# Right half of row blocks 2 and 3 as a streamed Strassen pair, with later loads of blocks 8 and 9 and a re-ordered second group

## Chip, cores, metric

One core of one Trainium2 chip. The metric is the device time of one execution in microseconds (us), as median over several executions. "Fast runs" are the undisturbed ones; all runs told of here are of that state, with every core's granted TensorE clock between 0.977 and 0.994.

## The reference

```python
def reference(a, b, gamma, eps):          # a, b: 2048 x 2048 float32, gamma: 2048
    x = np.matmul(a, b)
    rms = np.sqrt(np.mean(x ** 2, axis=-1, keepdims=True) + eps)
    return (gamma * x / rms).astype(np.float32)
```

The kernel works on 16 row blocks of 128 rows. Each row block of the output is finished only when all its 2048 columns exist, because the root mean square needs the whole row.

## The kernel before

The kernel has three phases.

1. **Streams.** A of row blocks 0 to 3 and the left half of B come in; each B block is used as it lands (first stream). Then the right half of B comes in the same way (second stream). Both are plain products.
2. **Strassen groups.** From row block 4 on, two row blocks form a group, and the group's left and right halves of 1024 columns each take seven products instead of eight. A product is 8 matmuls of 512 columns. While a group is computed, the next two row blocks of A are prepared: loaded, normed and scaled to fp16, transposed by DMA.
3. The last group is ordered by hand.

The parts that matter here:

```python
    def row_norm(mb):                       # ScalarE, 2.57 us
        for h in range(2):
            nc.scalar.activation(out=junk, in_=a32[mb][:, h * HALF:(h + 1) * HALF],
                                 func=ACTF.Square, scale=2.0 ** -8, accum_out=n2[:, h:h + 1])
        nc.scalar.activation(out=norm[mb], in_=n2[:, 0:1], func=ACTF.Sqrt, ...)
    # row_factor(mb): four small VectorE operations on norm[mb]
    # row_apply(mb):  a16 = a32 * factor, ScalarE for mb >= 6 (1.99 us); then transpose_dma(mb)
    # finish(mb):     VectorE: out = x * r * gamma, two half rows of 1.24 us, each stored by DMA

    def group_half(g, j, hooks):
        ...                                 # x11 .. x22: the four 512-column parts of the output
        t = x22
        at_hook(0)
        p2, p5 = new_bank(), new_bank()
        product(g, j, 2, p2)
        c = spare if (g, j) == (G0, 0) else t
        nc.scalar.copy(out=c, in_=p2)       # "the first copy"
        last_squares()
        at_hook(1)
        product(g, j, 5, p5)
        nc.vector.tensor_tensor(out=t, in0=p5, in1=c, op=ALU.add)
        at_hook(2)
        p1 = new_bank()
        product(g, j, 1, p1)
        ...
        at_hook(3)
        product(g, j, 4, p2, start=False)   # accumulates on p2: has to wait for the first copy
        nc.scalar.copy(out=x21, in_=p2)
        ...                                 # products 3, 7, 6 with hooks 4 to 7

    def hooks_of(g, j):                     # g == 2 is the first group, nxt = 2 * g + 2
        if j == 0:
            if g == G0: ...
            else:
                done = [2 * g - 2, 2 * g - 1]
                hook(0, row_factor, nxt)
                hook(1, apply, nxt)
                if g == G0 + 1:
                    hook(2, finish, r3)
                    done.insert(0, r3)
                for mb in done:
                    hook(1, take_rms, mb)
                hook(1, row_norm, nxt + 1)
                hook(2, row_factor, nxt + 1)
                hook(4 if g == G0 + 1 else 3, finish, 2 * g - 2)
                hook(4, apply, nxt + 1)
        else:
            ...
            if g + 2 < NG:
                hook(0, load_after, g, nxt + 2)     # waits for the first half's last sum
                hook(0, load_block, nxt + 3)
                hook(5, row_norm, nxt + 2)          # ahead of the next group's first copy
```

A hook is a place between two products at which the listed calls are issued. "Block 8" means row block 8 of A, and "scaling" a block is `row_apply`. The A sums are VectorE's sums of quarters of two row blocks of A; products 1, 2, 5, 6 and 7 of a group read them, so they need both blocks' transposes.

## Time and profile before

| | before |
|---|---|
| median | 224.36 us (224.12 to 224.77) |
| span of the profiled execution | 222.6 us, clock 0.993 |
| PE (TensorE matmul) busy | 211.1 us, 95% |
| DVE (VectorE) / ACT (ScalarE) busy | 73% / 58% |
| chain that ended last | PE 83%, DMA 8% |

The timeline of PE before, some of its rows. The columns are start, length, engine, source line, operation, output and input tiles, shape and count; a bracket at the end tells the idle time ahead of it and what ended it. A row without a bracket began as soon as the one before it let it.

```profile
24.69 1.67 PE L350 MATMUL acc<-b,head_at 128*128 128x512 bf16 x7 [0.44 <-DMA b<-in_b_dram]
...
69.25 3.62 PE L279 MATMUL acc<-b,s 128*128 128x512 bf16 x16
...
109.17 1.89 PE L279 MATMUL acc<-early,s 128*128 128x512 bf16 x8
110.90 3.62 PE L279 MATMUL acc<-early,head_at 128*128 128x512 bf16 x16
114.35 7.07 PE L279 MATMUL acc<-b,s 128*128 128x512 bf16 x32
```

The bracket at 24.69 is the last one; from there TensorE never waits. The first Strassen group starts at 69.25. The row at 110.90 is product 4 of the second group's right half: it follows its predecessor without a wait (it counts 16 matmuls because product 3 follows at once and stands in the same row).

ScalarE before, in the same stretch:

```profile
93.92 1.06 ACT L209 ACTIVATE sq<-a 128x1024 bf16<-128x1024 f32 x1 [1.33 <-DMA a<-in_a_dram]
...
96.49 0.57 ACT L498 COPY x<-acc 128x512 f32<-128x512 f32 x1
...
98.34 1.99 ACT L231 ACTIVATE head_at<-a,s 128x2048 f16<-128x2048 f32 x1
100.23 0.37 ACT L318 ACTIVATE rms<-tot 128x1 f32<-128x1 f32 x3
100.51 1.04 ACT L209 ACTIVATE sq<-a 128x1024 bf16<-128x1024 f32 x1
...
107.64 0.59 ACT L498 COPY x<-acc 128x512 f32<-128x512 f32 x1
```

The norm of block 8 (L209) waits for its load, but stands ahead of the first copy (L498 at 96.49). Scaling block 8 (L231 at 98.34) has no idle time ahead of it. The second half's first copy ends at 108.23, 2.7 us before product 4 needs it. That is the slack of this order.

### The profile page before, as it was taken

The page shows a single profiled execution, that of the slowest core. Times are in us where ns is not written, and L with a number is a line of the kernel's source. Part 1 is how long each engine was busy: PE and PEld are TensorE (multiplying, and loading weights), DVE is VectorE, ACT ScalarE, POOL GpSimd, SP SyncE. Part 2 cuts the span into 40 slices and gives each one's busy share as a digit, 9 for nine tenths or more (in the row PEclk, how much of TensorE's full clock was granted, in tenths as well). Part 3 has the DMA queues.
Part 4 walks back from the last instruction along what each step waited for, and adds up shares of the span by engine and source line. Part 5 has one row for each costly group of instructions (what it writes and reads, how often), then busy time and mean ns, then how long its engine had stood idle before and what let it go on. Part 6 is the DMA issues. An engine that isn't in the chain of part 4 may idle for free.

```text
span 222.6 us, 3026 instructions
## 1 busy us (share of the span) xinstructions
PE 211.1 (95%) x1043; PEld 98.6 (44%) x1043; DVE 161.8 (73%) x324; ACT 129.1 (58%) x272; POOL 24.5 (11%) x49
## 2 busy tenths in 40 slices
PE   7899999999999999999999999999999999999950
PEld 2445444444454444444444444444444444444430
DVE  2427557983999989978949298837994589587692
ACT  3110002807698895799646985699478954334570
POOL 7534232300000001000100002000200000000000
PEclk9999999999999999999999999999999999999997
DMA  6999999999973499818889259945994794044045
GB/s 184 223 202 209 203 208 211 212 303 259 327 280 159 188 272 292 310 72 226 276 228 400 58 174 222 366 151 143 246 368 168 97 282 189 0 188 193 0 190 188
DMA packets 36176, 47.13 MB, mean 212 GB/s; under 512 B 21952, under 2 KB 26048, under 8 KB 34496
## 3 DMA queue, kind: packets, MB, share of 16 engines
q0 software_dynamic: 9648, 23.33, 41.6%
q1 hardware_dynamic: 26080, 22.29, 33.0%
q10 hardware_dynamic: 432, 1.31, 2.0%
q8 instruction: 8, 0.13, 0.2%
q14 instruction: 8, 0.07, 0.1%
HBM read 34.60 MB, written 16.78 MB: 231 GB/s over the span
## 4 chain that ended last, share of the span: by engine, by line
PE 83%; DMA 8%; DVE 2%; POOL 2%; issue 1%; ACT 1%; DVEq 0%; ACTq 0%; POOLq 0%
PE acc L279 63%; PE acc L350 18%; DMA b<-in_b_dram 8%; POOL early L106 1%; DVE x L617 1%; POOL b L100 1%; DVE x L620 1%; PE tbank L179 1%; PE tbank L382 1%; PE tbank L165 1%; ACT sq L291 0%; DVEq L732 0%; ACT sq L682 0%; DVE x L690 0%; DVE r L322 0%
## 5 line engine op out<-in xcount | busy, mean ns | idle before, releaser
L279 PE MATMUL acc<-b,s 128*128 128x512 bf16 x376 | 83.3, 379 | 0.0
L279 PEld LDWEIGHTS <-s 128*128 128x128 f16 x472 | 46.2, 98 | 55.7 <-DVE s L244 0.2
L350 PE MATMUL acc<-b,head_at 128*128 128x512 bf16 x240 | 55.1, 379 | 0.6 <-DMA b<-in_b_dram 0.4
L291 ACT ACTIVATE sq<-x 128x512 bf16<-128x512 f32 x62 | 39.1, 631 | 10.9 <-DVE x L520 5.1
L340 DVE SCALAR_TENSOR_TENSOR x<-x,r,gamma_sb 128x1024 f32<-128x1024 f32 x28 | 34.7, 1282 | 0.8
L209 ACT ACTIVATE sq<-a 128x1024 bf16<-128x1024 f32 x24 | 25.4, 1057 | 16.8 <-DMA a<-in_a_dram 16.4
L350 PEld LDWEIGHTS <-head_at 128*128 128x128 bf16 x240 | 22.9, 98 | 26.7 <-issue 1.1
L393 ACT COPY x<-acc 128x512 f32<-128x512 f32 x11 | 5.9, 591 | 25.1 <-PE acc L350 25.1
L231 ACT ACTIVATE head_at<-a,s 128x2048 f16<-128x2048 f32 x10 | 19.9, 1990 | 0.0
L279 PEld LDWEIGHTS <-at_even 128*128 128x128 f16 x96 | 9.4, 98 | 11.5 <-issue 0.4
L279 PEld LDWEIGHTS <-head_at 128*128 128x128 f16 x96 | 9.4, 98 | 11.3
L100 POOL DMA_DIRECT2D b<-in_b_dram x15 | 10.6, 708 | 16.0 <-DMA b<-in_b_dram 13.2
L217 DVE TENSOR_SCALAR s<-norm 128x1 f32<-128x1 f32 x12 | 1.8, 150 | 14.3 <-ACT norm L212 14.2
L244 DVE TENSOR_TENSOR s<-at_even 128x1024 f16<-128x1024 f16 x15 | 9.7, 684 | 2.8 <-DMA at_even<-head_at 2.8
L291 ACT ACTIVATION_READ_ACCUMULATOR sq<-x 128x1 f32 x62 | 11.7, 188 | 0.0
L279 PE MATMUL acc<-t_left,s 128*128 128x512 bf16 x48 | 11.3, 379 | 0.0
L279 PE MATMUL acc<-early,s 128*128 128x512 bf16 x48 | 11.3, 379 | 0.0
L279 PE MATMUL acc<-early,at_even 128*128 128x512 bf16 x48 | 11.0, 379 | 0.0
L279 PE MATMUL acc<-t_left,at_even 128*128 128x512 bf16 x48 | 10.9, 379 | 0.0
L509 ACT COPY x<-acc 128x512 f32<-128x512 f32 x10 | 5.7, 575 | 8.9 <-PE acc L279 8.9
L279 PE MATMUL acc<-t_left,head_at 128*128 128x512 bf16 x48 | 10.8, 379 | 0.0
L279 PE MATMUL acc<-early,head_at 128*128 128x512 bf16 x48 | 10.8, 379 | 0.0
(86 smaller groups left out, 205.8 us busy)
## 6 DMA issues: line engine op xcount, KB each, us to landing
out_dram<-x SPq DMA_DIRECT2D x30, 512.0 KB, 3.1
a<-in_a_dram POOLq DMA_DIRECT2D x12, 1024.0 KB, 8.5
b<-in_b_dram POOLq DMA_DIRECT2D x15, 512.0 KB, 17.1
early<-in_a_dram POOLq DMA_DIRECT2D x7, 256.0 KB, 14.8
early<-in_b_dram ACTq DMA_DIRECT2D x2, 512.0 KB, 5.9
gamma_sb<-in_gamma_dram POOLq DMA_DIRECT2D x1, 1024.0 KB, 19.9
out_dram<-x SPq DMA_DIRECT2D x3, 256.0 KB, 3.5
early<-in_a_dram SPq DMA_DIRECT2D x1, 512.0 KB, 5.7
```

Of the source, the lines that this page charges most:

```text
L100: nc.gpsimd.dma_start(out=raw[j][kp], in_=b[kp * W2:(kp + 1) * W2, j * HALF:(j + 1) * HALF].rearrange("(t p) n -> p t n", p=P))
L106: nc.gpsimd.dma_start(out=ah(kp), in_=a[0:HB * P, kp * W2:(kp + 1) * W2].rearrange("(r p) k -> p r k", p=P))
L165: nc.tensor.matmul(view[:, t, r, :], ah(kp)[:, r, t * P:(t + 1) * P], identity, is_transpose=True, start=(t == 0 and r == 0), stop=(t == 1 ...
L209: nc.scalar.activation(out=junk, in_=a32[mb][:, h * HALF:(h + 1) * HALF], func=ACTF.Square, scale=2.0 ** -8, accum_out=n2[:, h:h + 1])
L231: nc.scalar.activation(out=a16[mb], in_=a32.pop(mb), func=ACTF.Copy, scale=factor.pop(mb))
L244: nc.vector.tensor_tensor(out=s_sum[s], in0=x, in1=y, op=op)
L279: nc.tensor.matmul(bank, lhsT[:, kp, :], rhs, start=(start and kp == 0), stop=(kp == KP - 1), skip_group_check=not start)
L291: nc.scalar.activation(out=sq[:, 0:CH], in_=src, func=ACTF.Square, scale=inv_sqrt_n, accum_out=msq[mb][:, c:c + 1])
L340: nc.vector.scalar_tensor_tensor(out=x, in0=x, scalar=r, in1=gamma_sb[:, h * HALF:(h + 1) * HALF], op0=ALU.mult, op1=ALU.mult)
L350: nc.tensor.matmul(bank, head_at[:, kt, r, :], head_rhs(c, kt), start=(kt == 0), stop=(kt == KT - 1))
L393: copy(out=x_chunk(*g), in_=banks[g])
L509: nc.scalar.copy(out=x21, in_=p2)
```

## The change

Its intent: save eight matmuls. Row blocks 2 and 3 times the right half of B become one Strassen pair, streamed with B: products 2, 5 and 1 are computed block by block as B lands, products 4, 3, 7, 6 after that. To make room, other work is moved:

- all of B is loaded ahead of A of blocks 4, 5;
- the pair's last sums and more finishes fall into the first group, so row block 2 is finished later;
- the loads of blocks 8, 9 wait for row block 2's scaling, not for the first half's last sum;
- block 8's norm, factor and scaling stand in the second group, behind its first copy; its factor stands behind row block 3's finish on VectorE.

The core of the diff (the streaming itself, many buffers and small moves are cut):

```diff
-    groups2 = [(r, c) for r in range(HB) for c in (2, 3)][:-1]
+    plain = [(r, c) for r in range(2) for c in (2, 3)]
+    ...
+    def stream_right(kp):                    # 8 plain matmuls and 3 of the pair per B block
+        ...
+    product(PAIR, 1, 4, pair[2], start=False)
+    product(PAIR, 1, 3, pair[5], start=False)
+    product(PAIR, 1, 7, p7, within={5: [lambda: turn(HB, 0)]})
+    product(PAIR, 1, 6, p6)
@@ group_half
-        t = x22
+        first = (g, j) == (G0, 0)
+        c, t = spare if first else (x22, x22)     # spare: now two buffers, one is t_first
@@ load_after
-        wait_for(x_chunk(2 * g + 1, 1)[:, 0:1])
+        wait_for(x_slot[r2][:, 0:1] if g == G0 else x_chunk(2 * g + 1, 1)[:, 0:1])
@@ hooks_of, second group, left half
+            elif g == G0 + 1:
+                hook(1, row_norm, nxt)
+                for mb in (r3, 2 * g - 2, 2 * g - 1):
+                    hook(1, take_rms, mb)
+                hook(2, finish, r3)
+                hook(2, row_factor, nxt)
+                hook(2, apply, nxt)
+                hook(2, row_norm, nxt + 1)
+                hook(3, row_factor, nxt + 1)
+                hook(4, finish, 2 * g - 2)
+                hook(4, apply, nxt + 1)
@@ hooks_of, right half
-                hook(0, load_after, g, nxt + 2)
-                hook(0, load_block, nxt + 3)
-                hook(5, row_norm, nxt + 2)
+                hook(2 if g == G0 else 0, load_after, g, nxt + 2)
+                hook(2 if g == G0 else 0, load_block, nxt + 3)
+                if g > G0:
+                    hook(5, row_norm, nxt + 2)
```

More of the change, by code (lines that the diff above doesn't have):

```diff
@@ L50 @@
     sq_pool = ctx.enter_context(tc.tile_pool(name="sq_pool", bufs=1))
-    stat_pool = ctx.enter_context(tc.tile_pool(name="stat_pool", bufs=8))
+    stat_pool = ctx.enter_context(tc.tile_pool(name="stat_pool", bufs=4))
+    msq_pool = ctx.enter_context(tc.tile_pool(name="msq_pool", bufs=8))
     ps_t = ctx.enter_context(tc.tile_pool(name="ps_t", bufs=1, space=bass.MemoryType.PSUM))
@@ L75 @@
     x_slot = [consts.tile([P, HALF], FP32, name=f"x_{n}") for n in range(8)]
-    spare = head_at.rearrange("p t r m -> p (t r m)")[:, K:2 * K].bitcast(FP32)[:, 0:CH]
+    spare = head_at.rearrange("p t r m -> p (t r m)")[:, K:2 * K].bitcast(FP32)
+    spare = [spare[:, 0:CH], consts.tile([P, CH], FP32, name="t_first")]
     def a16_slot(mb):
-        if mb < HB + 2:
-            return x_slot[HB + 1 + 2 * (mb % 2)].bitcast(FP16)
         flat = head_at.rearrange("p t r m -> p (t r m)").bitcast(FP16)
@@ L111, with load_half @@
     a32 = {}
+    def load_half(mb, h):
+        if h == 0:
+            a32[mb] = a_pool.tile([P, K], FP32, name="a32")
+        nc.gpsimd.dma_start(out=a32[mb][:, h * HALF:(h + 1) * HALF],
+                            in_=a[mb * P:(mb + 1) * P, h * HALF:(h + 1) * HALF])
     def load_block(mb):
@@ L123 @@
     load_head(1)
-    identity_f = consts.tile([P, P], FP32, name="identity_f")
+    identity_f = t_left[:, 2, KP - 1, 0:2 * P].bitcast(FP32)
     make_identity(nc, identity_f)
@@ L129 @@
     nc.vector.memset(warm, 0.0)
+    nc.vector.memset(pace, 1.0)
+    nc.scalar.activation(out=pace, in_=pace, func=ACTF.Sqrt)
     identity = consts.tile([P, P], BF16, name="identity")
@@ L172, with transpose_half @@
     a16 = {}
-    def transpose_half(mb, g):
-        bank = ps_t.tile([P, CH], FP32, name="tbank")
+    def transpose_half(mb, g, own_bank):
+        if own_bank:
+            bank = ps_t.tile([P, CH], FP32, name="tbank")
+        else:
+            bank = ps_a.tile([P, CH], FP32, name="acc")
         view = bank.bitcast(FP16).rearrange("p (g m) -> p g m", m=P)
@@ L182, in transpose_half, with take_transposed @@
             )
-        nc.vector.tensor_copy(out=at(mb)[:, g * 8:(g + 1) * 8, :], in_=view)
+        return view
+    def take_transposed(mb, g, view, copy):
+        copy(out=at(mb)[:, g * 8:(g + 1) * 8, :], in_=view)
     def transpose_dma(mb):
@@ L192, in new_msq @@
     def new_msq(mb):
-        msq[mb] = stat_pool.tile([P, NCH + 1], FP32, name="msq")
+        msq[mb] = msq_pool.tile([P, NCH + 1], FP32, name="msq")
         n_sq[mb] = 0
@@ L197 @@
         new_msq(mb)
+        nc.gpsimd.memset(msq[mb][:, NCH - 1:NCH], 0.0)
         nc.gpsimd.memset(msq[mb][:, NCH:], float(eps))
@@ L235, in quarter, with sum_of, a_sums @@
     def quarter(g, r, c):
+        if g < G0:
+            return head_at[:, c::2, 2 * g + r, :]
         return at(2 * g + r)[:, c::2, :]
-    def a_sums(g, which):
+    def sum_of(g, s):
+        return s_sum[s].bitcast(BF16) if g < G0 else s_sum[s]
+    def a_sums(g, which, lo=0, hi=KP):
         a11, a12, a21, a22 = (quarter(g, r, c) for r in range(2) for c in range(2))
@@ L243, in a_sums @@
             x, y, op = terms[s]
-            nc.vector.tensor_tensor(out=s_sum[s], in0=x, in1=y, op=op)
+            nc.vector.tensor_tensor(out=sum_of(g, s)[:, lo:hi, :], in0=x[:, lo:hi, :],
+                                    in1=y[:, lo:hi, :], op=op)
     def b_quarter(j, kp, r, c):
@@ L254, in b_sums @@
             nc.vector.tensor_tensor(out=sums[j][:, n, kp, :], in0=x, in1=y, op=op)
-    def b_sum_7(j, kp):
-        b21, b22 = (b_quarter(j, kp, 1, c) for c in range(2))
-        nc.vector.tensor_tensor(out=b21, in0=b21, in1=b22, op=ALU.add)
-    def b_sum_6(j, kp):
-        b11, b12 = (b_quarter(j, kp, 0, c) for c in range(2))
-        nc.vector.tensor_tensor(out=b12, in0=b12, in1=b11, op=ALU.add)
     def b_sums_in_place(j, kp):
@@ L270, in b_sums_in_place, with product_matmul, product @@
                                 op=ALU.add)
-    def product(g, j, m, bank, start=True):
-        for kp in range(KP):
-            lhsT = {3: quarter(g, 0, 0), 4: quarter(g, 1, 1)}[m] if m in (3, 4) else s_sum[m]
-            rhs = {1: lambda: sums[j][:, 0, kp, :], 2: lambda: b_quarter(j, kp, 0, 0),
-                   3: lambda: sums[j][:, 1, kp, :], 4: lambda: sums[j][:, 2, kp, :],
-                   5: lambda: b_quarter(j, kp, 1, 1), 6: lambda: b_quarter(j, kp, 0, 1),
-                   7: lambda: b_quarter(j, kp, 1, 0)}[m]()
-            nc.tensor.matmul(bank, lhsT[:, kp, :], rhs,
-                             start=(start and kp == 0), stop=(kp == KP - 1),
-                             skip_group_check=not start)
+    def product_matmul(g, j, m, bank, kp, start=True):
+        lhsT = {3: quarter(g, 0, 0), 4: quarter(g, 1, 1)}[m] if m in (3, 4) else sum_of(g, m)
+        rhs = {1: lambda: sums[j][:, 0, kp, :], 2: lambda: b_quarter(j, kp, 0, 0),
+               3: lambda: sums[j][:, 1, kp, :], 4: lambda: sums[j][:, 2, kp, :],
+               5: lambda: b_quarter(j, kp, 1, 1), 6: lambda: b_quarter(j, kp, 0, 1),
+               7: lambda: b_quarter(j, kp, 1, 0)}[m]()
+        nc.tensor.matmul(bank, lhsT[:, kp, :], rhs,
+                         start=(start and kp == 0), stop=(kp == KP - 1),
+                         skip_group_check=not start)
+    def product(g, j, m, bank, start=True, within={}):
+        for kp in range(KP):
+            for work in within.get(kp, ()):
+                work()
+            product_matmul(g, j, m, bank, kp, start)
     x_half = {}
@@ L291, in square, with square_half @@
         nc.scalar.activation(out=sq[:, 0:CH], in_=src, func=ACTF.Square,
+                             scale=inv_sqrt_n, accum_out=msq[mb][:, c:c + 1])
+    def square_half(mb, h):
+        c = n_sq[mb]
+        n_sq[mb] += 1
+        sq = sq_pool.tile([P, 2 * CH], BF16, name="sq")
+        nc.scalar.activation(out=sq, in_=x_tile(mb, h), func=ACTF.Square,
                              scale=inv_sqrt_n, accum_out=msq[mb][:, c:c + 1])
@@ L332, in rows @@
         return out[mb * P:(mb + 1) * P, lo:hi]
+    inverse_of = {}
     def finish(mb, order=(0, 1)):
-        if mb not in rms_of:
-            take_rms(mb)
-        r = inverse(rms_of.pop(mb))
+        if mb not in inverse_of:
+            if mb not in rms_of:
+                take_rms(mb)
+            inverse_of[mb] = inverse(rms_of.pop(mb))
+        r = inverse_of[mb]
         for h in order:
@@ L354, in new_bank @@
         return ps_a.tile([P, CH], FP32, name="acc")
-    later = ([("b", kp) for kp in range(5)]
-             + [("a", HB), ("b", 5), ("b", 6), ("a", HB + 1), ("b", 7)])
+    later = [("b", kp) for kp in range(KP)] + [("a", n) for n in range(4)]
     def load_later(n):
@@ L361, in load_later @@
             kind, which = later.pop(0)
-            load_b(1, which) if kind == "b" else load_block(which)
+            load_b(1, which) if kind == "b" else load_half(HB + which // 2, which % 2)
     def stream(groups, kp, before=(), when=None):
@@ L393, in evict @@
             copy(out=x_chunk(*g), in_=banks[g])
+    PAIR = G0 - 1
     groups1 = [(r, c) for r in range(HB) for c in range(2)][:-1]
@@ L399 @@
         x_tile(r, 0)
+    early_sums = {4: ((2,), 0, 6), 5: ((5,), 0, 7), 6: ((1,), 0, KP)}
     transpose_first()
@@ L406 @@
         before = [lambda: transpose_head(kp + 1)] if kp + 1 < KP else []
+        if kp in early_sums:
+            before.append(lambda: a_sums(PAIR, *early_sums[kp]))
         stream(groups1, kp, before, len(groups1) + 5 if kp == 0 else None)
@@ L412 @@
             b_sums(0, kp - 1)
+        if 0 < kp < KP - 2:
+            b_sums_in_place(0, kp - 1)
     load_later(2)
-    b_sums(0, KP - 1)
-    def prepare(mb):
-        row_norm(mb)
-        row_factor(mb)
-        row_apply(mb)
-    def b_sums_2(kp):
-        b_sums_in_place(0, kp)
-        b_sums(1, kp)
-        if kp + 1 < KP:
-            b_sum_7(1, kp)
-    r3 = HB - 1
-    squares = groups1 + [last1]
-    groups2 = [(r, c) for r in range(HB) for c in (2, 3)][:-1]
+    squares = groups1 + [last1]
@@ new lines, with pair_matmul @@
+    plain = [(r, c) for r in range(2) for c in (2, 3)]
+    pair = {}
+    def pair_matmul(m, kp):
+        if kp == 0:
+            pair[m] = new_bank()
+        product_matmul(PAIR, 1, m, pair[m], kp)
+    def stream_right(kp):
+        order = [(g, kt) for kt in (2 * kp, 2 * kp + 1) for g in plain]
+        if kp in (0, KP - 1):
+            order.sort(key=lambda x: plain.index(x[0]))
+        if kp == KP - 1:
+            for m in (2, 5):
+                pair_matmul(m, kp)
+            pair_matmul(1, kp - 1)
+        for g, kt in order:
+            if kt == 0:
+                banks[g] = new_bank()
+            head_matmul(banks[g], *g, kt)
+        if kp < KP - 1:
+            for m in (2, 5):
+                pair_matmul(m, kp)
+            if kp > 0:
+                pair_matmul(1, kp - 1)
+        else:
+            pair_matmul(1, kp)
@@ L431 @@
     for kp in range(KP):
         load_later(1)
-        before = [lambda: transpose_half(HB, 0)] if kp == 6 else []
-        if kp == 7:
-            before = [lambda: transpose_half(HB, 1)]
-        stream(groups2, kp, before)
+        b_sums(1, kp)
+        stream_right(kp)
         square(squares[kp][0], x_chunk(*squares[kp]))
-        if kp == 4:
-            prepare(HB)
-        if kp == 6:
-            prepare(HB + 1)
-        elif kp == KP - 1:
-            b_sums_in_place(0, kp - 1)
-        else:
-            b_sums_2(kp)
+        if kp > 0:
+            b_sums_in_place(1, kp - 1)
@@ L447 @@
+        if kp == 0:
+            b_sums(0, KP - 1)
+            b_sums_in_place(0, KP - 3)
+        if kp == 1:
+            b_sums_in_place(0, KP - 2)
+            b_sums_in_place(0, KP - 1)
+        if kp == 2:
+            a_sums(PAIR, (2,), 6, KP)
+            a_sums(PAIR, (5,), 7, KP)
+        if kp in (3, 4):
+            a_sums(PAIR, ((7, 6)[kp - 3],))
     nc.gpsimd.dma_start(out=gamma_sb, in_=gamma.partition_broadcast(P))
@@ L449, with turn, pair_sums, pair_ends @@
     load_block(HB + 3)
-    def squares2(r):
-        for c in (2, 3):
-            square(r, x_chunk(r, c))
-    evict(groups2[0:2], ())
-    squares2(0)
-    evict(groups2[2:-1], ())
-    bank = new_bank()
-    for kt in range(KT):
-        if kt in (0, 6):
-            transpose_half(HB + 1, kt // 6)
-            if kt == 0:
-                b_sums(1, KP - 2)
-                b_sum_7(1, KP - 2)
-        head_matmul(bank, r3, 3, kt)
-    evict(groups2[-1:], ())
-    row_norm(HB + 2)
-    a_sums(G0, (2, 5, 1))
-    finish(0, (1, 0))
-    b_sums_2(KP - 1)
-    nc.scalar.copy(out=x_chunk(r3, 3), in_=bank)
-    squares2(1)
+    r2, r3 = HB - 2, HB - 1
+    for r in range(HB):
+        x_tile(r, 1)
+    x11, x12, x21, x22 = (x_chunk(r, c) for r in (r2, r3) for c in (2, 3))
+    nc.scalar.copy(out=x22, in_=pair[2])
+    nc.vector.tensor_tensor(out=x22, in0=pair[5], in1=x22, op=ALU.add)
+    evict(plain, (2, 3))
+    b_sums_in_place(1, KP - 1)
+    product(PAIR, 1, 4, pair[2], start=False)
+    row_norm(HB)
+    row_norm(HB + 1)
+    nc.vector.tensor_tensor(out=x22, in0=pair[1], in1=x22, op=ALU.subtract)
+    row_factor(HB)
+    product(PAIR, 1, 3, pair[5], start=False)
+    row_apply(HB)
+    nc.scalar.copy(out=x21, in_=pair[2])
+    row_factor(HB + 1)
+    row_apply(HB + 1)
+    p7 = new_bank()
+    turned = {}
+    def turn(mb, g):
+        turned[mb, g] = transpose_half(mb, g, g == 0)
+    product(PAIR, 1, 7, p7, within={5: [lambda: turn(HB, 0)]})
+    turn(HB, 1)
+    for g in range(2):
+        take_transposed(HB, g, turned[HB, g], nc.scalar.copy)
+    nc.scalar.copy(out=x12, in_=pair[5])
+    p6 = new_bank()
+    product(PAIR, 1, 6, p6)
+    a_sums(G0, (5,))
+    for g in range(2):
+        turn(HB + 1, g)
+        take_transposed(HB + 1, g, turned[HB + 1, g], nc.vector.tensor_copy)
+    square_half(0, 1)
+    square_half(1, 1)
+    take_rms(0)
+    a_sums(G0, (2, 1))
+    def pair_sums():
+        nc.vector.tensor_tensor(out=x11, in0=x22, in1=x21, op=ALU.add)
+        nc.vector.tensor_tensor(out=x22, in0=x22, in1=x12, op=ALU.add)
+    def pair_ends():
+        nc.vector.tensor_tensor(out=x11, in0=p7, in1=x11, op=ALU.add)
+        nc.vector.tensor_tensor(out=x22, in0=p6, in1=x22, op=ALU.add)
     late = []
@@ L491, in group_half @@
         x11, x12, x21, x22 = (x_chunk(ra, c1), x_chunk(ra, c2), x_chunk(rb, c1), x_chunk(rb, c2))
-        t = x22
+        first = (g, j) == (G0, 0)
+        c, t = spare if first else (x22, x22)
         at_hook(0)
         p2, p5 = new_bank(), new_bank()
-        product(g, j, 2, p2)
-        c = spare if (g, j) == (G0, 0) else t
-        nc.scalar.copy(out=c, in_=p2)
+        one, two = ((5, p5), (2, p2)) if first else ((2, p2), (5, p5))
+        product(g, j, *one)
+        nc.scalar.copy(out=c, in_=one[1])
         last_squares()
         at_hook(1)
-        product(g, j, 5, p5)
-        nc.vector.tensor_tensor(out=t, in0=p5, in1=c, op=ALU.add)
+        product(g, j, *two)
+        nc.vector.tensor_tensor(out=t, in0=two[1], in1=c, op=ALU.add)
         at_hook(2)
@@ L550, in hooks_of @@
             if g == G0:
-                hook(0, row_factor, nxt)
-                hook(1, row_norm, nxt + 1)
-                hook(1, apply, nxt)
+                hook(0, finish, 0, (1,))
+                hook(1, row_norm, nxt)
+                hook(1, take_rms, 1)
+                hook(2, row_factor, nxt)
+                hook(2, finish, 0, (0,))
+                hook(2, apply, nxt)
+                hook(2, row_norm, nxt + 1)
                 hook(2, a_sums, g, (7, 6))
+                hook(2, finish, 1, (1, 0))
                 hook(2, row_factor, nxt + 1)
-                hook(2, finish, 1)
-                hook(3, squares2, 2)
+                hook(2, pair_sums)
+                hook(2, pair_ends)
                 hook(4, apply, nxt + 1)
-                hook(4, finish, 2)
-                hook(6, b_sum_7, 1, KP - 1)
+                hook(7, square_half, r2, 1)
+            elif g == G0 + 1:
+                hook(1, row_norm, nxt)
+                for mb in (r3, 2 * g - 2, 2 * g - 1):
+                    hook(1, take_rms, mb)
+                hook(2, finish, r3)
+                hook(2, row_factor, nxt)
+                hook(2, apply, nxt)
+                hook(2, row_norm, nxt + 1)
+                hook(3, row_factor, nxt + 1)
+                hook(4, finish, 2 * g - 2)
+                hook(4, apply, nxt + 1)
             else:
@@ L564, in hooks_of @@
                 hook(1, apply, nxt)
-                if g == G0 + 1:
-                    hook(2, finish, r3)
-                    done.insert(0, r3)
                 for mb in done:
@@ L571, in hooks_of @@
                 hook(2, row_factor, nxt + 1)
-                hook(4 if g == G0 + 1 else 3, finish, 2 * g - 2)
+                hook(3, finish, 2 * g - 2)
                 hook(4, apply, nxt + 1)
@@ L575, in hooks_of @@
             if g == G0:
-                hook(1, squares2, r3)
-                for kp in range(KP):
-                    hook(2, b_sum_6, 1, kp)
+                hook(1, take_rms, r2)
+                hook(1, square_half, r3, 1)
+                hook(2, finish, r2)
             else:
```

## The prediction

> **What bounds the kernel now.** TensorE. In the timeline its matmuls run from 24.69 us to 209.5 us with no idle time; the chain of waits is 83% PE. Seven 512-column matmuls take 1.51 us, 216 ns each, which agrees with the Trainium skill, "TensorE: Matmul & The Clock Gate", section "Wait — 56ns, not 53.3ns?" (215.7 ns warm). The page's clock row is at full speed.
>
> **What the change does to TensorE.** Row blocks 2, 3 times the right half become one Strassen pair: 7 products of 8 matmuls for 64 matmuls. 8 matmuls fewer: -1.73 us, if nothing new waits.
>
> **What else moves.**
> - The second stream consumes a B block per 11 matmuls (2.37 us) instead of 14 (3.02 us). GpSimd's waits for landings show one B block per about 2.5 us (38.9, 41.4, 43.9). B now comes before blocks 4, 5, so I estimate the last lands at 56.3 us, TensorE wanting it at 56.2: 0 to 0.3 us of waiting.
> - VectorE in that stream: per block 3 sums (1.02 us) plus in-place sums (0.61): full until about 61 us. Then row_factor (0.75) and row_apply (1.2) of block 4: about 63.5, wanted by TensorE's transposes at 63.35. Wait 0.2 to 0.5 us.
> - First group: two Strassen ends, three finishes (1.24 us a half row) and A sums before bank releases; I count 0.2 to 0.5 us of waits.
> - A table load (1.28 us, as in "ScalarE: Activation LUTs", "What ACT_TABLE_LOAD costs") moves to the start; it was not on the critical path. Worth 0.
>
> **The step I expect to cost.** In the second group block 8's norm (2.57 us ScalarE) now stands after the first product's copy, and its row_apply stands behind the finish of row block 3 on VectorE. ScalarE's order is: copy, two squares, norm 8, roots, [wait: reciprocal, finish 2.5, factor 0.75], apply 8 (1.9), norm 9 (2.57), copy, square, apply 9 (1.9), copy, square, copy of the second half's first product. I add 17.9 to 18.3 us from the end of the group's first product. TensorE has nine products of 1.727 us = 15.5 us until product 4 of the second half, which accumulates into the bank that last copy reads. So it waits 2.3 to 2.8 us. Before, the same copy came at 107.64, product 4 at 110.90. Apply 9 and its transpose come later too (the before kernel's A sums waited for it until 116.41, 0.7 us to spare): another 0 to 1.2 us.
>
> **Sum.** 224.36 - 1.73 + 0.6 + 2.6 + 0.5 = 226.3. I move this a little towards the case in which the queue has slack that I miss (then 222.8 to 223.6): 225.8 us, 80% range 222.9 to 227.4. Faster by over 2%: 0.01; within 2%: 0.94; slower by over 2%: 0.05.
>
> **What would show it.** 8 fewer 512-column matmuls; the first group after the streams starting at 67.5 to 68.3 us instead of 69.25; a PE wait of 2 to 3 us on ScalarE's copy of the second half's first product near 110 us, with ScalarE idle about 3 us for row_factor just before apply 8 near 100 us.
>
> **What would make it wrong.** ScalarE's chain shorter than summed (block 8 landing and norm early, or shorter waits for VectorE): then about 223. Waits of B or the bank releases larger than read: then over 227.

## The result

The changed kernel takes 226.64 us (226.19 to 227.35, 4 runs) beside 224.37 us (4 runs) of the kernel before on the same chip. The ratio is 1.0104, 95% interval 1.0081 to 1.0126. Ratios here are the mean time of one kernel's fast runs over that of the other's in the same rounds, so not quite the ratio of the medians. The profiled execution is the fastest of the four: span 224.4 us, clock 0.990. Its span is 1.8 us longer than before's.

The chain that ended last is now PE 72%, DMA 11%, DVE 6%, ACT 4%. PE after; the rows answer those of before:

```profile
24.67 1.67 PE L377 MATMUL acc<-b,head_at 128*128 128x512 bf16 x7 [0.28 <-DMA b<-in_b_dram]
...
67.55 3.73 PE L289 MATMUL acc<-b,s 128*128 128x512 bf16 x16
...
107.37 1.89 PE L289 MATMUL acc<-early,s 128*128 128x512 bf16 x8
111.12 3.61 PE L289 MATMUL acc<-early,head_at 128*128 128x512 bf16 x16 [1.86 <-ACT x L571]
114.57 3.62 PE L289 MATMUL acc<-b,s 128*128 128x512 bf16 x16
119.56 3.63 PE L289 MATMUL acc<-b,s 128*128 128x512 bf16 x16 [1.37 <-DVE s L264]
```

The first group starts 1.70 us earlier (67.55, was 69.25): the eight matmuls fewer are there, and the second stream waits for nothing. Then two new waits: product 4 of the second group's right half waits for ScalarE's copy (L571), and the next group's product waits for the A sums (L264).

How much do they cost? Without a wait, a row of 8 matmuls is followed after 1.73 us and one of 16 after 3.45 us. So the row at 111.12 should have stood at 109.10 (2.02 us late), and the row at 119.56 at 118.02 (1.54 us late). The sum is -1.70 + 2.02 + 1.54 = +1.86 us, and the spans differ by 1.8.

ScalarE after:

```profile
93.76 0.59 ACT L571 COPY x<-acc 128x512 f32<-128x512 f32 x1 [3.84 <-PE acc L289]
...
95.75 1.06 ACT L223 ACTIVATE sq<-a 128x1024 bf16<-128x1024 f32 x1
...
98.32 0.37 ACT L341 ACTIVATE rms<-tot 128x1 f32<-128x1 f32 x3
101.70 2.00 ACT L246 ACTIVATE head_at<-a,s 128x2048 f16<-128x2048 f32 x1 [3.01 <-DVE s L233]
...
110.50 0.57 ACT L571 COPY x<-acc 128x512 f32<-128x512 f32 x1
```

ScalarE idles 3.84 us ahead of the first copy (TensorE has to end the product), then does the norm of block 8 that before was done in that time, then idles 3.01 us for block 8's factor. VectorE tells why the factor is late:

```profile
98.74 2.48 DVE L367 SCALAR_TENSOR_TENSOR x<-x,r,gamma_sb 128x1024 f32<-128x1024 f32 x2
101.13 0.15 DVE L231 TENSOR_SCALAR s<-norm 128x1 f32<-128x1 f32 x1
101.31 0.16 DVE L232 RECIPROCAL s<-s 128x1 f32<-128x1 f32 x1
101.51 0.15 DVE L233 TENSOR_SCALAR s<-s 128x1 int32<-128x1 int32 x1
...
118.81 1.90 DVE L264 TENSOR_TENSOR s<-at_even 128x1024 f16<-128x1024 f16 x3 [2.96 <-DMA at_even<-head_at]
```

The factor (L231 to L233) needs a norm that was ready at 98.4 (ScalarE's square root at 98.12, 0.29 us long), but stands behind 2.48 us of row block 3's finish. The last row is the other wait: the A sums wait for block 9's transpose. The trace's DMA records show that transpose issued at 110.71 and landed at 118.78; before, it was issued at 108.41 and landed at 116.38. Its time in flight is the same (8.0 and 8.1 us), but its issue is 2.3 us later. In both kernels it is issued directly behind the second store of row block 4; that store follows row block 4's finish, which started at 105.47 before and at 107.78 after, because on VectorE it stands, in both kernels, behind block 9's factor, and that now waits 3.77 us for block 9's late norm (the factor started at 103.19 before and at 106.29 after).

### The profile page after: what moved, and what is told of

Read it like the earlier page. It is cut to its first block, busy times and chain, and to the rows that moved or that the text cites. A ratio compares the mean times of both kernels' runs of the same rounds, so it can differ in the third digit from the quotient of the medians.

```text
span 224.4 us, 3015 instructions
## 1 busy us (share of the span) xinstructions
PE 210.0 (94%) x1035; PEld 97.6 (43%) x1035; DVE 168.0 (75%) x330; ACT 127.5 (57%) x263; POOL 26.6 (12%) x55
## 4 chain that ended last, share of the span: by engine, by line
PE 72%; DMA 11%; DVE 6%; ACT 4%; POOL 2%; issue 2%; DVEq 0%; ACTq 0%; POOLq 0%
PE acc L289 58%; PE acc L377 12%; DMA b<-in_b_dram 8%; DMA at_even<-head_at 4%; DVE x L367 2%; ACT sq L223 2%; POOL early L105 1%; DVE x L703 1%; POOL b L99 1%; ACT sq L307 1%; ACT head_at L246 1%; DVE x L706 1%; PE tbank L408 1%; PE tbank L172 1%; PE tbank L189 0%
## 5 line engine op out<-in xcount | busy, mean ns | idle before, releaser
L289 PE MATMUL acc<-b,s 128*128 128x512 bf16 x408 | 92.3, 379 | 1.4 <-DVE s L264 1.4
L289 PEld LDWEIGHTS <-s 128*128 128x128 f16 (+1 forms) x512 | 49.8, 98 | 61.5 <-DVE s L264 2.3
L377 PE MATMUL acc<-b,head_at 128*128 128x512 bf16 x176 | 41.9, 379 | 0.4 <-DMA b<-in_b_dram 0.3
L307 ACT ACTIVATE sq<-x 128x512 bf16<-128x512 f32 x54 | 34.0, 630 | 8.9 <-DVE x L593 3.3
L377 PEld LDWEIGHTS <-head_at 128*128 128x128 bf16 x176 | 16.8, 98 | 20.1 <-issue 1.3
L419 ACT COPY x<-acc 128x512 f32<-128x512 f32 x6 | 3.4, 586 | 25.0 <-PE acc L377 25.0
L289 PEld LDWEIGHTS <-head_at 128*128 128x128 f16 (+1 forms) x112 | 10.9, 98 | 15.3 <-issue 2.1
L289 PE MATMUL acc<-early,head_at 128*128 128x512 bf16 x64 | 14.5, 379 | 1.9 <-ACT x L571 1.9
L231 DVE TENSOR_SCALAR s<-norm 128x1 f32<-128x1 f32 x12 | 1.8, 151 | 16.7 <-ACT norm L226 16.7
L264 DVE TENSOR_TENSOR s<-head_at 128x1024 f16<-128x1024 f16 (+5 forms) x22 | 13.4, 637 | 0.1
L264 DVE TENSOR_TENSOR s<-at_even 128x1024 f16<-128x1024 f16 x15 | 9.8, 686 | 4.5 <-DMA at_even<-head_at 4.1
L280 DVE TENSOR_TENSOR b<-b 128x1024 bf16<-128x1024 bf16 x16 | 10.9, 689 | 0.2
```

The costliest lines, as they stand in the source:

```text
L264: nc.vector.tensor_tensor(out=sum_of(g, s)[:, lo:hi, :], in0=x[:, lo:hi, :], in1=y[:, lo:hi, :], op=op)
L280: nc.vector.tensor_tensor(out=flat[:, 1:3, :], in0=flat[:, 1:3, :], in1=flat[:, 0::3, :], op=ALU.add)
L289: nc.tensor.matmul(bank, lhsT[:, kp, :], rhs, start=(start and kp == 0), stop=(kp == KP - 1), skip_group_check=not start)
L307: nc.scalar.activation(out=sq[:, 0:CH], in_=src, func=ACTF.Square, scale=inv_sqrt_n, accum_out=msq[mb][:, c:c + 1])
L377: nc.tensor.matmul(bank, head_at[:, kt, r, :], head_rhs(c, kt), start=(kt == 0), stop=(kt == KT - 1))
L419: copy(out=x_chunk(*g), in_=banks[g])
```

## The experiments

Theory A at the start: the streamed pair itself is worth its 1.7 us; the order of the second group, and block 8's later loads, cost more. Rivals: B, the later loads or changed DMA traffic cost; C, the pair's own sums cost VectorE time that shows later.

The first four ran on one chip (before: 224.27 us), the other seven on another (224.34; 224.37 with one more run for the last three). No run is labelled e7. Diffs are against the changed kernel where nothing else is said.

### e1: the norm of block 8 back in the first group

```diff
@@ hooks_of
+                # second group: factor of block 8 at hook 0, scaling at hook 1, as before
-                hook(1, row_norm, nxt)
+                hook(0, row_factor, nxt)
+                hook(1, apply, nxt)
@@
-                if g > G0:
-                    hook(5, row_norm, nxt + 2)
+                hook(5, row_norm, nxt + 2)
```

> The changed kernel with block 8's norm, factor and apply put back where the kernel before has them (norm at the end of the first group, apply right after the second group's first copy); the later loads stay. Theory A (the new order in the second group makes TensorE wait 1.9 us for ScalarE's copy, and a further 1.4 us because block 9's transpose lands late): the 1.9 us wait near 110 us is gone; block 8 lands at about 94 us, so the norm just fits; block 9's transpose is issued near 108.3 us and lands near 116.4, TensorE wants the sums at 115.9, so a wait of 0.7 to 1.5 us stays. Time 223.5 to 224.4 us. Rival B (the later loads of blocks 8 and 9 cost): no change, 226.3 to 227. Rival C (the streamed Strassen pair with its extra VectorE work costs): no change.

Measured: 226.35 us (225.92 to 226.66), ratio 1.0087 [1.0075, 1.0099]. A miss. ScalarE:

```profile
96.02 1.06 ACT L223 ACTIVATE sq<-a 128x1024 bf16<-128x1024 f32 x1 [6.05 <-DMA a<-in_a_dram]
...
98.58 0.56 ACT L571 COPY x<-acc 128x512 f32<-128x512 f32 x1
```

PE:

```profile
99.20 5.32 PE L289 MATMUL acc<-t_left,head_at 128*128 128x512 bf16 x16 [1.97 <-ACT x L571]
```

Block 8's load, issued at 88.84, has landed only at 96. A norm ahead of the first copy now holds the copy up until 98.58, and TensorE waits for it (1.97 us). So the new place of the norm was not chosen badly: with these loads, a norm ahead of the copy costs about as much as one behind it. The cost had only moved.

One thing more showed. The 16 matmuls after that wait took 5.32 us instead of 3.6, at half clock for one stretch of 3.4 us. It cannot be what made this version slow: the other four runs had a mean clock of 0.993 or 0.994, against 0.982 in the profiled one, and took 225.92 to 226.66 us beside its 226.48. What they lost in its place is not recorded. An estimate from this trace: block 9's transpose landed at 118.61, and the first of the three sums that read it (1.90 us together) was ready at about 119.26. TensorE, held up by the half clock, wanted it only at 119.89; 1.7 us (5.32 - 3.62) earlier it would have waited about 1 us there. The half clock asked for a test of its own (e11, e12).

### e2: the loads back, the norm as in the changed kernel

```diff
-        wait_for(x_slot[r2][:, 0:1] if g == G0 else x_chunk(2 * g + 1, 1)[:, 0:1])
+        wait_for(x_chunk(2 * g + 1, 1)[:, 0:1])
@@
-                hook(2 if g == G0 else 0, load_after, g, nxt + 2)
-                hook(2 if g == G0 else 0, load_block, nxt + 3)
+                hook(0, load_after, g, nxt + 2)
+                hook(0, load_block, nxt + 3)
```

> The changed kernel with only the load wait of blocks 8 and 9 put back (after the first half's last sum, 84.9 us in the changed kernel's trace, instead of row block 2's finish at 87.5). ScalarE did not wait for block 8 in the changed kernel, so theory A: no change, 226.2 to 227.2 us, both waits (1.9 on the copy, 1.4 on the sums) still there. Rival B: faster by 1.5 us or more. Rival C: no change.

Measured: 231.22 us (230.56 to 231.5), ratio 1.0302 [1.0288, 1.0317]. A clear miss, and in a direction that neither theory had: earlier loads cost 4.6 us. ScalarE:

```profile
98.66 0.58 ACT L571 COPY x<-acc 128x512 f32<-128x512 f32 x1 [8.85 <-DMA out_dram<-x]
```

The first copy waits 8.85 us for a store. It writes into `x_6`, from which row block 2's right half is still being stored. The DMA records:

| | loads of blocks 8, 9 issued | `x_6`'s store issued | landed | in flight |
|---|---|---|---|---|
| before | 88.37, 88.90 | 85.95 | 89.66 | 3.7 us |
| changed kernel | 88.78, 89.31 | 88.83 | 92.96 | 4.1 us |
| e2 | 85.50, 86.03 | 88.72 | 98.56 | 9.8 us |

In e2 a store of 512 KB that was issued some three microseconds behind two loads of 1 MB landed after both (the loads at 90.75 and 96.94). (The Trainium skill, "DMA: Bandwidth & Descriptors", section "Issuing engines are not separate DMA queues", says that DMAs run on the same 16 engines whichever engine issued them. This run agrees: the loads were issued by GpSimd, the stores by SyncE.) In the changed kernel the store is issued with the loads and lands at 92.96, before the product ends at 93.6. So the new load wait lets the store through in time. Rival B, as I had put it (later loads cost), has fallen. (The profiled execution of e2 also had two stretches at half clock, as in e1. The other three runs had mean clocks of 0.982 to 0.987 against its 0.977 and took 230.56 to 231.5 us beside its 231.31, so these stretches are not what made e2 slow.)

### e3: both back

The diffs of e1 and e2 together.

> The changed kernel with both put back: what is left is the streamed Strassen pair and its first group. Theory A: block 8 lands near 91 us, its norm fills ScalarE's idle time before 93.8 us, everything after comes about 2.5 us earlier, block 9's transpose is issued before 107 us and lands before the loads of blocks 10 and 11 start; no TensorE wait after 25 us, 222.4 to 223.0 us (224.37 - 1.73). Rival B alone: like the loads put back alone. Rival C: still 225 or more.

Measured: 226.15 us (225.61 to 226.42), ratio 1.0076 [1.0064, 1.0089]. A miss again:

```profile
91.14 1.06 ACT L223 ACTIVATE sq<-a 128x1024 bf16<-128x1024 f32 x1 [1.07 <-DMA a<-in_a_dram]
...
99.05 0.58 ACT L571 COPY x<-acc 128x512 f32<-128x512 f32 x1 [5.25 <-DMA out_dram<-x]
```

```profile
99.69 1.89 PE L289 MATMUL acc<-t_left,head_at 128*128 128x512 bf16 x8 [2.36 <-ACT x L571]
```

The norm of block 8 is now early, as hoped, but the copy waits for the store, and TensorE for the copy (2.36 us). From here on the theory is A': **the parts are tied to each other.** The pair's late sums delay row block 2's finish (83.19 before, 86.32 after) and its stores; the second group's first copy needs the stored buffer; therefore the loads have to wait; therefore block 8's norm has to stand behind the copy; and that lengthens ScalarE's order. A' says where to cut: either repair the order of the second group (e4, e6, e8), or free the copy of the buffer (e9, e10).

### e4: block 8's factor ahead of row block 3's finish

```diff
-                hook(2, finish, r3)
                 hook(2, row_factor, nxt)
+                hook(2, finish, r3)
                 hook(2, apply, nxt)
```

> The changed kernel, block 8's norm still in the second group, but its row_factor (0.75 us on VectorE) ahead of row block 3's finish (2.5 us). Theory A: ScalarE's 3.0 us of idle time before apply 8 falls to 0.9, its chain is 2.2 to 2.5 us shorter, the copy comes near 108.6 us and the 1.9 us wait goes; the transpose of block 9 lands near 116 to 117, so 0.5 to 1.4 us of wait for the sums may stay. Time 223.8 to 224.9 us. If instead the norm's own 2.6 us of ScalarE was the whole of it: a wait of over 1 us stays on the copy and the time is over 225.3. Rivals B and C: no change.

Measured: 223.65 us (223.33 to 224.55), ratio 0.9976 [0.9959, 0.9992]. Just outside: 0.15 us under the range, and far from what the alternative wants (over 225.3); the waits are as the theory has them. The rows that decide, ScalarE and PE:

```profile
99.36 2.00 ACT L246 ACTIVATE head_at<-a,s 128x2048 f16<-128x2048 f32 x1 [0.33 <-DVE s L233]
```

```profile
25.00 1.67 PE L377 MATMUL acc<-b,head_at 128*128 128x512 bf16 x7 [0.79 <-DMA b<-in_b_dram]
...
117.01 3.63 PE L289 MATMUL acc<-b,s 128*128 128x512 bf16 x16 [0.50 <-DVE s L264]
```

ScalarE's idle time ahead of block 8's scaling falls from 3.01 to 0.33 us; TensorE's wait for the copy is gone, the one for the A sums falls to 0.50. One line moved gives about 3 us of the changed kernel's 226.64 back (the two ran on different chips; the ratio fell by 0.0128, which is 2.9 us), and the result is already faster than the kernel before.

### e5: the kernel before, with the new order of the second group alone

The converse: no streamed pair, no late loads, but the changed kernel's hooks of the second group and no norm at hook 5 of the first.

```diff
+            elif g == G0 + 1:        # into the kernel before
+                hook(1, row_norm, nxt)
+                ...                  # as in the change
-                hook(5, row_norm, nxt + 2)
+                if g > G0:
+                    hook(5, row_norm, nxt + 2)
```

> The kernel before, with only the change's order of the second group (block 8's norm behind the first copy, its factor and row_apply behind row block 3's finish). Theory A' (the added waits come from that order alone, and not from the streamed pair): the copy of the second half's first product comes 17 to 18 us after the end of the group's first product, TensorE waits 1.5 to 2.5 us for it and again 1 to 1.5 us at the A sums, so 226.5 to 228.5 us, ratio 1.010 to 1.018. Rival (the order costs only because the pair's late ends and late loads come with it): 224.2 to 224.7, ratio 1.000.

Measured: 228.22 us (227.73 to 228.43), ratio 1.0169 [1.0155, 1.0183]. A hit. PE:

```profile
113.04 3.62 PE L279 MATMUL acc<-early,head_at 128*128 128x512 bf16 x15 [1.85 <-ACT x L498]
...
121.56 3.63 PE L279 MATMUL acc<-b,s 128*128 128x512 bf16 x16 [1.45 <-DVE s L244]
```

The same two waits, 1.85 and 1.45 us (1.86 and 1.37 in the changed kernel), in a kernel that has no streamed pair. So the pair is not needed for the loss: the order alone makes it. That removes rival C as the cause of these two waits; that the pair costs nothing elsewhere is shown by e9.

### e6: block 9's transpose ahead of row block 4's stores

```diff
-                hook(4, finish, 2 * g - 2)
                 hook(4, apply, nxt + 1)
+                hook(4, finish, 2 * g - 2)
```

> The changed kernel, with block 9's row_apply and transpose ahead of row block 4's finish, so that its transpose is queued ahead of that finish's two stores. Theory: the second PE wait (1.4 us at 119.6, for the A sums that read block 9's transpose) is there because the transpose stands behind those stores and then shares the DMA engines with the load of block 10; ahead of both it lands by about 114 and the second wait goes; the first wait (1.9 us for ScalarE's copy) stays: 224.8 to 225.6 us, ratio 1.003 to 1.006. Rival (block 9's row_apply itself is too late, the queue does not matter): as the changed kernel, 226.2 to 226.9.

Measured: 225.95 us (225.68 to 226.24), ratio 1.0071 [1.0059, 1.0083]. A miss on the time: between the two expectations, 0.35 us over the theory's range and 0.25 us under the rival's. The trace decides for the theory's cause. PE:

```profile
111.73 3.61 PE L289 MATMUL acc<-early,head_at 128*128 128x512 bf16 x15 [2.18 <-ACT x L571]
124.27 1.89 PE L289 MATMUL acc<-t_left,at_even 128*128 128x512 bf16 x7 [0.29 <-ACT x L571]
126.45 1.89 PE L289 MATMUL acc<-t_left,at_even 128*128 128x512 bf16 x8 [0.29 <-DVE x L575]
```

The wait for the A sums is gone: the transpose was issued at 110.01 and landed after 4.3 us, at 114.28. So the wait's cause was the transpose's place in the queue, behind the two stores. Of its 1.37 us, 0.58 came back as two small waits in the next group; the ratio fell by 0.0033, which is 0.74 us. (The wait for the copy is longer by 0.3 us here because in this execution block 8's load landed 0.36 us too late for its norm.)

### e8: both repairs

e4 and e6 together.

> The changed kernel with both repairs: block 8's factor ahead of row block 3's finish on VectorE, and block 9's transpose ahead of row block 4's stores. Theory: both waits gone, TensorE idle only at the start and under 0.5 us after it: the 8 matmuls fewer show in full, 222.4 to 223.3 us, ratio 0.991 to 0.995, below the 223.65 us of the version with the factor alone. Rival (the remaining 0.5 us wait has another cause, or a new wait comes for row block 4's late stores): 223.5 to 224.2.

Measured: 223.33 us (223.09 to 224.13), ratio 0.9959 [0.9945, 0.9973]. 0.03 us over the theory's range (in the ratio, 0.9959 beside 0.995), under the rival's. TensorE waits for 0.32 us of B at 24.66 and 0.29 us at 123.56, and no more that the profile brackets.

### e9: loads and norm back, and a buffer of its own for the first copy

e3, plus:

```diff
         c, t = spare if first else (x22, x22)
+        if (g, j) == (G0 + 1, 0):
+            c, t = spare[1], spare[1]      # t_first: free since the first group's first half
```

> The changed kernel with the loads and the norm both back (that version took 226.15 us), and with the second group's first copy and its sums in a buffer of their own, so that the copy need not wait for row block 2's store. Theory A' (the early loads cost because that store then lands late and the copy writes into its slot): ScalarE's wait of 5.25 us for the store goes, PE waits fall from 3 us to under 0.7, 222.5 to 223.5 us, ratio 0.992 to 0.996. Rival (early loads cost by DMA traffic as such): 225.6 to 226.4, as without the buffer. Possible in between: row block 4's fourth product still writes that slot 7 us later, and a store later than about 100 us would show there.

Measured: 222.62 us (222.47 to 223.27, 6 runs), ratio 0.9926 [0.9914, 0.9938]. A hit, and the fastest version. ScalarE, then PE:

```profile
90.84 1.06 ACT L223 ACTIVATE sq<-a 128x1024 bf16<-128x1024 f32 x1 [1.06 <-DMA a<-in_a_dram]
...
93.62 0.59 ACT L573 COPY t_first<-acc 128x512 f32<-128x512 f32 x1
...
105.70 0.59 ACT L573 COPY x<-acc 128x512 f32<-128x512 f32 x1 [1.06 <-PE acc L289]
```

```profile
24.47 1.67 PE L377 MATMUL acc<-b,head_at 128*128 128x512 bf16 x7 [0.25 <-DMA b<-in_b_dram]
...
108.96 3.62 PE L289 MATMUL acc<-early,head_at 128*128 128x512 bf16 x15
```

The same loads and the same norm as in e3, one buffer more: the 5.25 us wait for the store is gone (the store itself still lands as late, at 98.29, but `x_6` is next written at 100.20), and TensorE has no wait from 24.47 us on. The gain over the kernel before, 224.34 - 222.62 = 1.72 us, is that of the eight matmuls (8 x 0.216 = 1.73). This is what the streamed pair is worth when nothing else is lost.

### e10: the loads back and the buffer, the norm behind the copy

e2 plus the two lines of e9.

> The changed kernel with the loads back (that version took 231.22 us), its norm of block 8 still behind the first copy, and the second group's first copy and sums in a buffer of their own. Theory A' (the early loads cost only through the slot that the copy writes into): the 8.85 us wait for the store goes; the order of the second group still costs what it costs in the changed kernel, a PE wait of 1.8 to 2.3 us at 111 us and up to 1.4 us at 119.5: 225.9 to 226.9 us, ratio 1.007 to 1.011. Rival (early loads cost by themselves): over 229.

Measured: 226.47 us (226.38 to 226.52), ratio 1.0093 [1.0078, 1.0108]. A hit. ScalarE, then PE:

```profile
101.73 2.00 ACT L246 ACTIVATE head_at<-a,s 128x2048 f16<-128x2048 f32 x1 [3.01 <-DVE s L233]
```

```profile
111.15 3.61 PE L289 MATMUL acc<-early,head_at 128*128 128x512 bf16 x15 [1.86 <-ACT x L573]
...
119.89 3.63 PE L289 MATMUL acc<-b,s 128*128 128x512 bf16 x16 [1.68 <-DVE s L264]
```

Beside e2 the buffer is worth 2.1% (1.0302 to 1.0093), so the early loads cost through that buffer. And what stays is the loss of the order: ScalarE idles 3.01 us ahead of block 8's scaling, PE waits 1.86 and 1.68 us. With e9 the pair of runs splits the two causes: with the buffer and the early loads, the order of the second group alone (block 8's norm, factor and scaling, and what follows from them) makes 226.47 or 222.62.

### e11, e12: a wait of a known length

Both are e9 plus a wait put in on purpose. In the right half of the third group the second product has to wait until ScalarE, after its first copy, has rewritten some of that product's own weights in place with the same values.

```diff
         nc.scalar.copy(out=c, in_=one[1])
+        if (g, j) == (G0 + 2, 1):
+            nc.scalar.copy(out=s_sum[5][:, 0:1, :], in_=s_sum[5][:, 0:1, :])     # e11
+            # e12: three times nc.scalar.copy(out=s_sum[5], in_=s_sum[5])
```

> The version without waits (222.62 us), with one wait put in on purpose: in the second half of the third Strassen group the second product has to wait until ScalarE has copied the first product's bank and then 128 of its own columns in place. The wait is worked out at 1.0 to 1.3 us. Theory (a wait that fills under 45% of one 3.4 us window of the clock costs its own length): 223.5 to 224.0 us, no half-clock window after it. Rival (any wait slows the clock): over 224.8.

> As the version with the short wait, but three in-place copies of 1024 columns on ScalarE, so a wait of 3.7 to 4.1 us, which seldom covers a whole window of 3.4 us. Theory (a wait that fills more than some 55% of a window halves the clock in the next one, which costs up to 1.7 us more): 227.6 to 228.6 us, one half-clock window behind the wait in the profile, 16 matmuls at about 5.3 us in place of 3.6. Rival (only a wholly idle window slows the clock, which needs a lucky phase with this wait): 226.3 to 226.8 in most runs.

Measured: e11 223.75 us (223.72 to 223.87), ratio 0.9974 [0.9961, 0.9987]; e12 228.31 us (227.79 to 229.46, 6 runs), ratio 1.0188 [1.0164, 1.0213]. Both medians lie in the ranges; two of the six runs of e12 (229.35 and 229.46) lie above its range of 227.6 to 228.6. PE of e11, then of e12:

```profile
131.06 1.90 PE L289 MATMUL acc<-b,s 128*128 128x512 bf16 x8 [0.88 <-ACT s L575]
```

```profile
134.07 3.43 PE L289 MATMUL acc<-b,s 128*128 128x512 bf16 x8 [3.77 <-ACT s L576]
```

The short wait (0.88 us in the bracket, which counts a little less than the delay, as with the two waits of the changed kernel) cost 1.13 us and left the matmuls after it at 1.90 us for eight. The long one (3.77 us) cost 5.69 us, and the eight matmuls after it took 3.43 us: the clock record shows half clock from 133.80 to 137.21.

In this profiled execution the wait happened to cover one of the clock's 3.4 us windows as a whole (130.39 to 133.80), so the profile alone does not decide between the theory and the rival. The other runs do: with a wait of 3.77 us a window lies wholly inside it in about (3.77 - 3.41) / 3.41 = 10% of the phases, but all six runs took at least 5.17 us more than e9's median, and their mean clocks were 0.978 to 0.986 beside e9's 0.987 to 0.993. And the profiles before had shown it with shorter waits:

| wait | idle share of one window | next window at half clock |
|---|---|---|
| after, 1.86 us at 111.12 | 36% | no |
| e3, 2.36 us at 99.69, which lay across two windows | 27%, 42% | no |
| e5, 1.45 us at 121.56 | 42% | no |
| e10, 1.86 us at 111.15 | 46% | no |
| e10, 1.68 us at 119.89 | 47% | no |
| e6, 2.18 at 111.73, across two windows | 32%, 32% | no |
| e1, e2 (two waits): 1.97, 2.23, 2.79 us | 58%, 65%, 80% | yes, all three |

(The shares come from laying a grid of 3.413 us through the times at which the clock record changes.) The bound lies between 47% and 58% of a window, if it is a share at all; nothing here shows it more closely. Neither the kernel before nor the changed one was hit by it in its profiled execution, so it does not explain the profiled difference. It is a danger that the change came near to.

### All of them

| version | us | ratio to before |
|---|---|---|
| before | 224.3 | 1 |
| changed kernel | 226.64 | 1.0104 |
| e1 norm back | 226.35 | 1.0087 |
| e2 loads back | 231.22 | 1.0302 |
| e3 both back | 226.15 | 1.0076 |
| e4 factor first | 223.65 | 0.9976 |
| e5 before, new order alone | 228.22 | 1.0169 |
| e6 transpose first | 225.95 | 1.0071 |
| e8 factor and transpose first | 223.33 | 0.9959 |
| e9 both back, own buffer | 222.62 | 0.9926 |
| e10 loads back, own buffer | 226.47 | 1.0093 |
| e11 e9 and a short wait | 223.75 | 0.9974 |
| e12 e9 and a long wait | 228.31 | 1.0188 |

## Why the prediction was right

It said 225.8 us, range 222.9 to 227.4; measured 226.64. Point by point:

- **Eight matmuls fewer, -1.73 us.** Right: the first group starts 1.70 us earlier, and e9 shows 1.72 us in the time.
- **B and VectorE in the second stream, the first group's bank releases: together +0.6 us.** Too much. No wait showed in the profiled execution between 24.67 and 111 us. That B is close is right all the same: one execution (e12) had a wait of 0.25 us for B at 56.54, where I had estimated that TensorE wants the last B block at 56.2 and that it lands at 56.3.
- **The wait for ScalarE's copy, 2.3 to 2.8 us near 110 us.** Right in place, releaser and cause; the row at 111.12 stood 2.02 us late, so the term was too large by some 0.5 us. ScalarE's idle time of 3 us ahead of block 8's scaling was 3.01, and e4 shows by taking it away that it was the cause.
- **Block 9's transpose, 0 to 1.2 us (0.5 in the sum).** Too small: 1.54 us. This is the term that was mis-sized. The prediction carried only that scaling block 9 and its transpose come later; the transpose is issued behind row block 4's stores, and these came 2.3 us later. Less the 0.7 us to spare that I had read, this gives 1.6. e6 shows it: with the transpose ahead of those stores its wait is gone.
- **The sum.** The terms gave 226.3, and I moved it to 225.8 for slack that I might have missed. There was none of that kind. The profiled terms, -1.70 + 2.02 + 1.54 = +1.86, are close to the +1.94 of the sum. That is partly luck: 0.6 us that did not come and some 0.6 us too much for the copy made up for 1.0 us too little for the transpose.
- **Left over.** The measured difference is 2.27 us (226.64 - 224.37), 0.4 more than the profiled execution shows. The four runs of the changed kernel had spans from 224.4 to 225.5, and the profiled one was the shortest; where the others lost up to 1.1 us more is not recorded. A stretch at half clock in some of them is not excluded: their mean clocks were 0.984 to 0.987 against its 0.990.

What the prediction did not see is why the change re-ordered the second group at all. I took the load wait and the norm's new place for two separate choices and my first experiments (e1 to e3) for two separate repairs; all three missed. They are one constraint, the buffer `x_6`, and it took e9 and e10 to show it.

## What to carry to other kernels

When work is saved on the bounding engine, follow what the saving makes later: here a finish came 3 us later, its store kept a buffer busy, and loads, a norm and a chain of another engine were re-ordered for that buffer's sake; one small buffer more, with the old loads and the old order back, gave back all that the re-ordering had cost (e9; the buffer without the old order did not, e10). Where an engine works in the order of the program, as VectorE does in these traces, put a short operation that another engine waits for ahead of a long one that no engine waits for so soon: moving four operations that end within 0.8 us ahead of a finish of 2.5 us was worth about 3 us (e4). And before undoing a part of a change, ask what that part is protecting: of the norm's place and the loads' wait, neither undone alone was a clear gain (e1, e2), and the second cost 4.6 us.

## What the Trainium skill lacked or had wrong

- "TensorE: Matmul & The Clock Gate", sections "What's actually happening" and "HAM oscillation — how this bites in real kernels": they put the return to the slow clock at one idle window of about 3.4 us, and give the rule "no PE-idle gaps >~3.4µs". Waits of 1.97, 2.23 and 2.79 us halved the clock for the next 3.4 us here, where they filled 58%, 65% and 80% of one window; waits that filled up to 47% of any window did not, one of 2.36 us among them. A wait of 3.77 us cost 5.69 us. The window's length agrees: the half-clock stretch was 133.80 to 137.21 us.
- "DMA: Bandwidth & Descriptors", section "Issuing engines are not separate DMA queues": what it says agrees, but it has no number for how long a small transfer can be held up by large ones issued ahead of it. A 512 KB store issued 2.7 us after the second of two 1 MB loads was in flight for 9.8 us (e2; 8.9 to 10.0 us in e3 and e9 to e12), against 2.65 us with no load about and 4.1 us when issued together with the loads.
- The same page, sections "DMA Transpose (X-bar)" and "Latency and other measured facts": neither has the time of one transpose from issue to landing, or what a queue ahead of it does to it. The transpose of one 128 x 2048 fp16 block took 4.25 to 4.3 us from issue to landing with nothing ahead of it. Issued right behind a store, its issue alone took 3.3 us in place of 1.7 to 1.9, and it landed after 5.1 us (e4, e8, block 8). Behind stores and with loads issued some 2 us after it, it took 7.6 to 8.4 us (block 9, in every version but e6 and e8).
